# A decoder trunk on one core: the first stage written out as one fixed sequence, and the first gate's products in two halves

## The chip, the core and the metric

The kernel runs on one core of a Trainium2 chip. TensorE (PE) multiplies, VectorE (DVE), ScalarE (ACT) and GpSimd (POOL) work on tiles, SyncE (SP) issues most of the transfers. The metric is the time of one execution on the device in microseconds (us), the median of several runs.

## The reference

Two layers, each with one mixer of three groups of heads side by side; x is 1024 tokens by 1024 channels in f32. What matters here is the beginning of a layer:

```python
mod = c_act @ w_mod + b_mod                      # c_act = SiLU(c), 1024 -> 3 * 1024
shift, scale, gate = jnp.split(mod[:, None, :], 3, axis=-1)
h = rms_norm(x, pre_gain) * (1.0 + scale) + shift
proj = h @ w_in                                  # columns of three groups of heads
...                                              # window attention, retention, gated linear attention
y = jnp.concatenate([a_out, r_out, g_out], axis=-1) @ w_out
return x + gate * rms_norm(y, post_gain)
```

Before any projection of the first layer can be multiplied, shift and scale must be there, and with them h for at least one tile of tokens.

## The kernel before

Tokens are cut into eight tiles of 128 (t), channels into eight of 128 (k). Every f32 operand of a projection is held as a high part and a low part (hi, lo); a product is three passes over the channels, hi by hi, lo by hi and hi by lo, so that a tile with one unit of 256 columns is 24 matmuls. The unit "gg" (the gate of the linear attention) carries 16 more columns, "ga", and has 272; "rg" is the gate of the retention. `project` makes a product, `do_gates` goes through gg and rg for a pair of tiles.

PE issues its instructions in the order in which the program emits them. The other engines' queues are ordered by a scheduler, except where `issue_after` holds an instruction behind another. A planner's clock (`clk`) decides what the program emits next: each matmul adds its cost (columns / 2400, at least 0.107 for 128 stationary columns; 0.109 for an f32 transpose), a generator (`job`) yields a delay and goes on at the first `pump` after it, and `await_flag` moves the clock on where something isn't due yet. The delays stand in the table `L`; `pump` is called every 7 matmuls.

The first stage (`mod_first`, with `between`) works on shift and scale of layer 0 in two halves of 512 channels (hh). For each half ten transfers bring the weights of shift (`wm[0]`) and scale (`wm[1]`), 4 MB for a half. Shift is a row product on PE (line 165 by `mult`, 128x512 operands with one stationary column); scale is summed on VectorE over eight k (L326, L328). `finish` turns both into columns: four matmuls with the summed scale, four with the copied row (L337), each as two instructions, then L309 to L311. Between the two halves stand the loading and splitting of gg (L527 hi on ScalarE, L533 lo on GpSimd, L540 and L541 for ga), and `pre` for tiles 0 and 1 with `early=True`: squares (L651), sum and power for the root (L640, L634, L635 on GpSimd), x times root (L666), eight transposes on PE (L180), modulation (L698 on ScalarE, L700 on VectorE), high part (L704) and low part (L687 or L708). `finish` of the first half is called within the second half's loop, at k = FIN = 1.

After it the jobs for tiles 2 and 3 (with a delay `L["pf1"]` = 6.35 ahead of their transposes) and 4 to 7 (`pre_first`: `L["pf3"] + L["pf2"] * (t - 4)` ahead of their squares, then `pre1` = 7.44 ahead of their transposes) are started, rg is loaded (after x of tiles 2 and 3 in SP's queue; hi on VectorE, lo on VectorE and for the last quarter on GpSimd), and `layer(0)` begins with `do_gates`: gg and rg for tiles 0 and 1, then for 2 and 3, and so on. A tile's product waits for its flag `hT`, which `pre` sets 3.0 after its last step.

Of the kernel before, what the change touches and what calls it, by code (L numbers as in the profile page):

```python
# [10 lines left out]
F32 = mybir.dt.float32  # L11
# [6 lines left out]
P = 128  # L18
# [75 lines left out]
def trunk(ctx: ExitStack, tc: tile.TileContext, ins, cst, out):  # L94
# [200 lines left out]
    def mod_first(rws, between):  # L295
        for j in range(2):
            mod_tile(0, j)
        rc = []
        shift, gain = modc[(0, 0)], modc[(0, 1)]

        def finish(hh, row, acc):
            pc = mm()
            for b in range(4):
                mult(pc[:, 4 + b:5 + b], acc[:, b * P:(b + 1) * P], ones[:, 0:1], True, True)
            for b in range(4):
                mult(pc[:, b:b + 1], row[0:1, b * P:(b + 1) * P], ones[0:1, 0:1], True, True)
            ks = slice(4 * hh, 4 * hh + 4)
            col = small(4)
            V.tensor_tensor(col, pc[:, 4:8], rc[1][:, ks], ALU.add)  # L309
            V.scalar_tensor_tensor(gain[:, ks], col, 1.0, rc[1][:, 8 + 4 * hh:12 + 4 * hh], ALU.add, ALU.mult)  # L310
            V.tensor_tensor(shift[:, ks], pc[:, 0:4], rc[0][:, ks], ALU.add)  # L311
            flag(("modh", 0, hh), 0.0)

        late = None
        for hh in range(2):
            wm = [wp.tile([P, KT, 512], F32, name=nm("wm")) for _ in range(2)]
            acc = t2()
            row = gp.tile([1, 512], F32, tag="acc", name=nm("row"), bufs=1)
            pm = mm()
            for k0, k1 in ((0, 2), (2, 4), (4, 6), (6, 7), (7, 8)):  # L320
                for j in range(2):
                    nc.sync.dma_start(wm[j][:, k0:k1, :], w_mod[0, j, hh, :, k0:k1, :])
            between(hh, -1)
            for k in range(KT):
                if k == 0:
                    V.tensor_scalar(acc, wm[1][:, k], c_act[:, k:k + 1], None, ALU.mult)  # L326
                else:
                    mark[2] = V.scalar_tensor_tensor(acc, wm[1][:, k], c_act[:, k:k + 1], acc, ALU.mult, ALU.add)  # L328
                mult(pm[0:1, :], c_act[:, k:k + 1], wm[0][:, k], k == 0, k == KT - 1)
                if hh == 0 and k == 3:  # L330
                    rc.extend(mod_rows_t(r_) for r_ in rws)
                if late is not None and k == FIN:
                    pump()
                    finish(0, *late)
                    pump()
                between(hh, k)
            A.activation(row, pm[0:1, :], AF.Copy)  # L337
            if hh == 0:
                late = (row, acc)
        finish(1, row, acc)  # L340
        pump()

    def mod_third(l, j):
# [164 lines left out]
    def load(l, name, first=None):  # L508
# [11 lines left out]
        def conv(kc, st):  # L520
            hi, lo = (wt[:, a, 2 * kc:2 * kc + 2, 0:256] for a in range(2))
            if name[0] == "o" and kc == 3:
                A.activation(hi, st, AF.Copy, scale=gnc[:, l:l + 1])
                V.scalar_tensor_tensor(lo, st, gnc[:, l:l + 1], f(hi), ALU.mult, ALU.subtract)
            else:
                if first == 0:
                    A.activation(hi, st, AF.Copy)  # L527
                elif first == 1:
                    V.tensor_copy(hi, st)
                else:  # L530
                    copy(f"whi{kc}", hi, st)
                e = G if first == 0 or name[0] == "o" and kc == 2 else eng(f"wlo{kc}")
                e.tensor_tensor(lo, st, f(hi), ALU.subtract)  # L533
            if kc == 3:
                if name == "gg":
                    gt = wt[:, :, :, 256:272]
                    st = t1()
                    sg = st[:, 0:128].rearrange("p (k n) -> p k n", k=KT)
                    nc.sync.dma_start(sg, w_ga[l])
# [4 lines left out]
        for kc in range(KT // 2):  # L544
            if first is not None:
                conv(kc, *issue(kc))
            else:
                request(l, 1, lambda kc=kc: issue(kc), lambda st, kc=kc: conv(kc, st))
# [83 lines left out]
    def rstd_of(ss, w, scale, eps):  # L632
        r = small(w)
        V.tensor_scalar(r, ss, scale, eps, ALU.mult, ALU.add)  # L634
        G.tensor_tensor(r, r, mhalf[:, :w], ALU.pow)  # L635
# [9 lines left out]
    mark = [None] * 4  # L645
    eb = []
# [7 lines left out]
    def pre(l, t, xt, early=False, soon=False):  # L654
# [12 lines left out]
        yield 0.5 if early else L["pf1"] if soon else lat("pre1", l)  # L667


        at = {}  # L670

        def turn(kt, bank, i):
            at[kt] = bank[:, i * P:(i + 1) * P]
            transp(at[kt], xn[kt // 4][:, kt % 4 * P:(kt % 4 + 1) * P], ident)

        if early:
            if not eb:
                eb.extend((aux(), aux()))
            x = aux()
            for kt in range(KT):  # L680
                turn(kt, x if kt < 4 else eb[kt // 6], kt if kt < 4 else 2 * t + kt % 2)
        late = []
        for j in range(2):
            yield (0.0, ("modh", l, j))
            if late:
                with tc.issue_after(mark[2].ins):
                    V.tensor_tensor(*late.pop(), ALU.subtract)  # L687
            if not early:
# [1033 lines left out]
```

## Time and profile before

| | |
|---|---|
| median of three runs | 998.06 us (997.43 to 999.33) |
| profiled execution | 996.31 us, span 994.6 us |
| granted TensorE clock, mean | 0.991 |
| busy: PE, DVE, ACT, POOL | 965.7, 683.2, 409.3, 246.3 us |
| moved by DMA | 148.77 MB, 150 GB/s over the span |

The span is from the first to the last instruction of the profiled execution; what lies around it is 1.7 us. Rows of the timeline give the start and the length in us, then engine, line, operation, tiles written and read, form, count, and in brackets the idle time of the engine before it and what ended that. Rows of the stretches give the length, then the busy time and the count of PE, PE's weight loads, DVE, ACT and POOL, then the granted clock, the share of the DMA engines and GB/s. Line 165 is the helper for every matmul, line 180 the one for every transpose, so the tiles tell which it is.

### The profile page before, as it was taken

How to read it: one execution, taken by the hardware profiler on the slowest of the kernel's cores; microseconds unless marked ns; L12 is line 12 of the kernel's file. 1: busy time of each engine (PE TensorE's matmuls, PEld its weight loads, DVE VectorE, ACT ScalarE, POOL GpSimd, SP SyncE). 2: the span in 40 equal slices, each digit the busy share in tenths (PEclk: the TensorE clock that was granted, in tenths of full speed). 3: DMA queues.
4: the chain of work that ended last, by engine and by line, in shares of the span. 5: the costliest groups of instructions: out<-in, count | busy, mean ns of one | idle time of the engine just before them, and what ended most of it. 6: DMA issues, size and time to landing. Idle time of an engine off the chain costs nothing.

```text
span 994.6 us, 19641 instructions
## 1 busy us (share of the span) xinstructions
PE 965.7 (97%) x7133; PEld 824.3 (83%) x7133; DVE 683.2 (69%) x1679; ACT 409.3 (41%) x1152; POOL 246.3 (25%) x310
## 2 busy tenths in 40 slices
PE   5899999999999999999999999999999999999996
PEld 1599999888998777778889999988999877777785
DVE  3779857677766777664677286775766577567876
ACT  2477312233332656632555332133333257574222
POOL 2322001233310234420124101113322034545000
PEclk8899999999999999999999999999999999999999
DMA  9843513523135355587555241352122434378883
GB/s 321 290 138 97 159 44 115 177 86 121 61 100 166 91 157 168 170 274 239 189 170 171 69 150 38 118 157 83 53 93 86 127 91 133 112 235 266 267 262 139
DMA packets 112305, 148.77 MB, mean 150 GB/s; under 512 B 12065, under 2 KB 63821, under 8 KB 112209
## 3 DMA queue, kind: packets, MB, share of 16 engines
q1 hardware_dynamic: 106512, 137.96, 44.5%
q10 hardware_dynamic: 5696, 9.56, 2.6%
q8 instruction: 56, 0.92, 0.4%
q14 instruction: 41, 0.33, 0.1%
HBM read 109.20 MB, written 36.18 MB: 146 GB/s over the span
## 4 chain that ended last, share of the span: by engine, by line
PE 80%; DVE 7%; DMA 7%; issue 2%; POOL 1%; ACT 1%; SPq 0%; ACTq 0%; POOLq 0%; DVEq 0%
PE mm L165 61%; PE aux L165 14%; PE aux L180 5%; DMA st<-in_w_in_dram 2%; POOL sm L635 1%; DMA t<-aoS 1%; DMA st<-in_w_last_dram 1%; DMA xk<-in_x_dram 1%; DVE arena L533 1%; DMA a<-mixS 1%; DVE t L1248 0%; DVE t L328 0%; DMA t<-in_x_dram 0%; DMA t<-xs 0%; DMA mixS<-t 0%
## 5 line engine op out<-in xcount | busy, mean ns | idle before, releaser
L165 PE MATMUL mm<-arena 128*128 128x256 f32 (+2 forms) x1824 | 299.9, 318 | 1.8 <-ACT arena L704 1.8
L165 PE MATMUL mm<-arena,arena 128*128 128x256 f32 (+2 forms) x1824 | 298.2, 316 | 0.0
L165 PEld LDWEIGHTS mm<-arena 128*128 128x128 f32 x1824 | 255.5, 191 | 26.0 <-issue 3.3
L165 PEld LDWEIGHTS mm<-arena,arena 128*128 128x128 f32 x1824 | 252.2, 188 | 24.3 <-issue 3.7
L635 POOL TENSOR_TENSOR sm<-sm,mhalf 128x1 f32<-128x1 f32 (+1 forms) x64 | 55.8, 872 | 335.9 <-DVE sm L634 317.8
L165 PE MATMUL mm<-arena,mx 128*128 128x512 f32 (+1 forms) x564 | 130.6, 387 | 0.5 <-ACT kept L1341 0.5
L165 PEld LDWEIGHTS mm<-arena,mx 128*128 128x128 f32 x564 | 101.4, 188 | 24.7 <-issue 1.9
L149 ACT ACTIVATE t<-aux 128x256 f32<-128x256 f32 (+2 forms) x124 | 55.8, 468 | 73.8 <-PE aux L180 62.2
L149 ACT ACTIVATE arena<-st 128x512 fp32r<-128x512 f32 x94 | 56.2, 627 | 53.2 <-DMA st<-in_w_in_dram 19.4
L929 POOL TENSOR_TENSOR smx<-smx,sm 128x512 f32<-128x512 f32 x32 | 36.1, 1129 | 125.7 <-DVE sm L928 118.0
L533 POOL TENSOR_TENSOR arena<-st,arena 128x512 fp32r<-128x512 f32 x31 | 42.7, 1378 | 79.7 <-ACT arena L149 72.9
L533 DVE TENSOR_TENSOR arena<-st,arena 128x512 fp32r<-128x512 f32 x77 | 58.0, 775 | 5.2 <-ACT arena L149 3.3
L925 ACT ACTIVATE smx<-smx,sm 128x129 f32<-128x129 f32 x128 | 49.9, 393 | 25.9 <-DVE sm L922 25.7
L364 DVE SCALAR_TENSOR_TENSOR acc<-st,c_act,acc 128x512 f32<-128x512 f32 x60 | 46.7, 778 | 16.9 <-DMA st<-in_w_mod_dram 16.5
L180 PE MATMUL aux<-c_ident,t 128*128 128x128 f32 (+1 forms) x292 | 48.2, 282 | 5.4 <-DVE t L666 5.0
L180 PEld LDWEIGHTS aux<-c_ident,t 128*128 128x128 f32 (+1 forms) x292 | 35.0, 144 | 12.4 <-DVE t L666 6.9
L698 ACT ACTIVATE t<-aux,mod,mod 128x128 f32<-128x128 f32 x68 | 25.9, 459 | 43.0 <-DVE t L1248 18.1
L165 PEld LDWEIGHTS aux<-t,mx 32*128 32x128 f32 (+1 forms) x896 | 39.5, 187 | 3.9 <-issue 2.1
L973 ACT ACTIVATE t<-aux 128x256 f32<-128x256 f32 x32 | 12.3, 383 | 73.6 <-PE aux L165 65.0
L165 PE MATMUL aux<-t,mx 32*128 32x32 f32 (+1 forms) x896 | 40.7, 272 | 0.0
L920 DVE COPY_PREDICATED smx<-c_curmask,aux 128x256 f32<-128x256 int32 x64 | 25.4, 446 | 19.5 <-ACT smx L149 17.2
L1248 DVE SCALAR_TENSOR_TENSOR t<-t,sm,t 128x512 f32<-128x512 f32 x32 | 24.0, 780 | 18.2 <-DMA t<-in_x_dram 10.8
(224 smaller groups left out, 1387.7 us busy)
## 6 DMA issues: line engine op xcount, KB each, us to landing
st<-in_w_in_dram SPq DMA_DIRECT2D x96, 256.0 KB, 3.8
st<-in_w_mod_dram SPq DMA_DIRECT2D x64, 256.0 KB, 3.1
mx<-mixS SPq DMA_DIRECT2D x20, 512.0 KB, 4.9
mixS<-t SPq DMA_DIRECT2D x72, 128.0 KB, 3.7
st<-in_w_last_dram SPq DMA_DIRECT2D x36, 256.0 KB, 3.8
wm<-in_w_mod_dram SPq DMA_DIRECT2D x12, 512.0 KB, 7.0
t<-in_x_dram SPq DMA_DIRECT2D x24, 256.0 KB, 4.9
t<-tabS SPq DMA_DIRECT2D x16, 256.0 KB, 4.6
```

Of the source, the lines that this page charges most:

```text
L149: A.activation(dst, src, AF.Copy)
L165: T.matmul(dst, lhsT, rhs, start=start, stop=stop)
L180: T.transpose(dst, src, idn)
L364: V.scalar_tensor_tensor(acc, wt, c_act[:, k:k + 1], acc, ALU.mult, ALU.add)
L533: e.tensor_tensor(lo, st, f(hi), ALU.subtract)
L635: G.tensor_tensor(r, r, mhalf[:, :w], ALU.pow)
L698: A.activation(hf[:, ks], at[kt], AF.Identity, scale=gain, bias=shift)
L920: V.copy_predicated(sv, curmask.unsqueeze(1).to_broadcast((P, 2, P)), pv[:, :, n // P - 1, :])
L925: A.activation(sm[:, h, :], sm[:, h, :], AF.Exp, bias=mx[:, h:h + 1], accum_out=sums[:, h:h + 1])
L929: eng("pn").tensor_tensor(sm[:, :, 0:128], sm[:, :, 0:128], rs.unsqueeze(2).to_broadcast((P, 4, P)), ALU.mult)
L973: A.activation(sq, po, AF.Square)
L1248: V.scalar_tensor_tensor(xt[j], yg[j], r, xt[j], ALU.mult, ALU.add)
```

## The change

The first stage becomes a function `first`, and stands in a region in which VectorE, ScalarE, GpSimd and SP, too, issue in the order in which the program emits them (`ORDERED`). Its steps are small functions, called one after the other: loads of half 0, gg, ga, half 1, then rg, then x of tiles 2 and 3 on SP; sums and row products in pairs of k; squares and normalisation of tiles 0 and 1 among them; tile 0's transposes ahead of the row products of k = 6, 7, tile 1's behind the first four column matmuls. The row is copied ahead of three of the four high parts of gg. All low parts of gg, of ga and of rg are GpSimd's; rg's high parts are two on ScalarE and two on VectorE, the latter after the second half's low parts. The low parts of the first half of the channels stand among the sums of the second half.

In `do_gates` the first pair's gg products are made in two halves of the channels: channels 0 to 3 of tile 0 and of tile 1 in two PSUM tiles, then channels 4 to 7 of each. `project` waits for the flag `hT` only where its last channel is among them, as before.

The delays are others: 7.0 and 8.5 for tiles 2 and 3 (`pf2`, `pf3`), 17.3 + 4.16 (t − 4) for the others (`pf4`, `pf5`); the flag `hT` of tiles 0 and 1 is set 2.6 after the last step, rg's flag 3.0 after. Three memsets on GpSimd (those of `acc` and of the two tiles in `gla_tiles`) are held behind the last power of tiles 2 and 3.

```diff
-    def mod_first(rws, between):
...
             if j == 2:
-                G.memset(acc, 0.0)
+                with tc.issue_after(mark[0].ins):
+                    G.memset(acc, 0.0)
...
-        G.tensor_tensor(r, r, mhalf[:, :w], ALU.pow)
+        mark[1] = G.tensor_tensor(r, r, mhalf[:, :w], ALU.pow)
...
-        yield L["pf3"] + L["pf2"] * (t - 4)
+        yield L["pf4"] + L["pf5"] * (t - 4)
         yield from pre(0, t, xt)
...
+    def first(wp):
...
+        def rest(t, j):
+            hi, lo = halves(t, j)
+            V.tensor_tensor(lo, hv[(t, j)], f(hi), ALU.subtract)
...
+        def wlo(n, kc, st):
+            G.tensor_tensor(w[n][:, 1, 2 * kc:2 * kc + 2, 0:256], st, f(w[n][:, 0, 2 * kc:2 * kc + 2, 0:256]),
+                            ALU.subtract)
+
+        mod_load(0)
+        gst = list(issue("gg"))
+        sg = ga_load(0)
+        mod_load(1)
+        sums(0, 0, 1)
+        rowp(0, 0, 1)
+        sums(0, 2, 3)
+        rowp(0, 2, 3)
+        sq(0)
+        rc = [mod_rows_t(r_) for r_ in rws]
+        rowp(0, 4, 5)
+        r0 = rstd2(ss[0])
+        norm(0, r0)
+        sq(1)
+        turn(0)
+        sums(0, 4, 5)
+        r1 = rstd2(ss[1])
+        sums(0, 6)
+        rowp(0, 6, 7)
+        sums(0, 7)
+        norm(1, r1)
+        whi("gg", 0, gst[0], A)
+        wlo("gg", 0, gst[0])
+        row_out(0)
+        pc = cols_a(0)
+        turn(1)
+        for kc in (1, 2, 3):
+            whi("gg", kc, gst[kc], A)
+            wlo("gg", kc, gst[kc])
+        gt = w["gg"][:, :, :, 256:272]
+        A.activation(gt[:, 0], sg, AF.Copy)
+        G.tensor_tensor(gt[:, 1], sg, f(gt[:, 0]), ALU.subtract)
+        cols_r(0, pc)
+        flag(("w", 0, "gg"))
+        modulate(0, 0)
+        modulate(1, 0)
+        rowp(1, 0, 1)
+        sums(1, 0, 1)
+        rest(0, 0)
+        rowp(1, 2, 3)
+        sums(1, 2, 3)
+        rest(1, 0)
+        rgen = issue("rg")
+        rst = [next(rgen) for _ in range(4)]
         for t in (2, 3):
+            load_x(t, xe[t], nc.sync)
+        rowp(1, 4, 5)
+        sums(1, 4, 5)
+        rowp(1, 6, 7)
+        sums(1, 6, 7)
+        row_out(1)
+        pc = cols_a(1)
+        yield
+        w["rg"] = unit(0, "rg")
+        for kc in (0, 1):
+            whi("rg", kc, rst[kc], A)
+            wlo("rg", kc, rst[kc])
+        cols_r(1, pc)
+        for t in range(2):
+            modulate(t, 1)
+        for t in range(2):
+            rest(t, 1)
+            flag(("hT", 0, t), 2.6)
+        for kc in (2, 3):
+            whi("rg", kc, rst[kc], V)
+            wlo("rg", kc, rst[kc])
+        flag(("w", 0, "rg"), 3.0)
+
+    with tc.manual_schedule(engines=ORDERED):
+        with tc.tile_pool(name="first", bufs=1) as wp:
+            steps = first(wp)
+            next(steps)
+        ap = ctx.enter_context(tc.tile_pool(name="big1", bufs=1))
+        arenas.append(ap.tile([P, 4 * SLOT], F32R, name="arena1"))
+        for _ in steps:
+            pass
+        for t in (2, 3):
+            job(pre(0, t, xe[t], f"pf{t}"))
         pump()
...
         def do_gates(name, p):
             w = used(l, name)
+            halved = {}
+            if l == 0 and p == 0 and name == "gg":
+                for t in range(2):
+                    halved[t] = mm()
+                    project(halved[t][:, 0:272], l, t, w, 272, range(KT // 2))
             for t in (2 * p, 2 * p + 1):
-                pg = mm()
+                pg = halved.get(t) or mm()
                 if name == "gg":
-                    project(pg[:, 0:272], l, t, w, 272)
+                    project(pg[:, 0:272], l, t, w, 272, range(KT // 2 if t in halved else 0, KT))
...
-L = {..., "pf3": 13.2, "pf1": 6.35, "pf2": 4.16, ...}
+L = {..., "pf2": 7.0, "pf3": 8.5, "pf4": 17.3, "pf5": 4.16, ...}
+ORDERED = {mybir.EngineType.DVE, mybir.EngineType.Activation, mybir.EngineType.Pool, mybir.EngineType.SP}
-FIN = 1
```

More of the change, by code (lines that the diff above doesn't have):

```diff
@@ L293, in mod_tile @@
         modc[(l, j)] = cp.tile([P, KT], F32, name=nm(f"mod{j}"), tag=f"mod{j}")
-    def mod_first(rws, between):
[L296 to L341, printed above, removed]
     def mod_third(l, j):
@@ L666, in pre @@
                 V.tensor_scalar(xn[j], xt[j], r, None, ALU.mult)
[L667 to L682, printed above, removed]
+        yield L[soon] if soon else lat("pre1", l)
         for j in range(2):
             yield (0.0, ("modh", l, j))
[L685 to L688, printed above, removed]
[L689 to L691 removed]
+            x = aux()
+            for k in range(4):
+                kt = 4 * j + k
+                transp(x[:, k * P:(k + 1) * P], xn[j][:, k * P:(k + 1) * P], ident)
             hf = t2()
```

157 lines of the change are left out of this document (101 added, 56 removed).

## The prediction

> **What bounds the kernel now.** I read the page first, then the chain of work that ended last, the timeline of TensorE, one-microsecond stretches, and single tiles.
>
> ```profile
> span 994.6 us, 19641 instructions
> ...
> PE 965.7 (97%) x7133; PEld 824.3 (83%) x7133; DVE 683.2 (69%) x1679; ACT 409.3 (41%) x1152; POOL 246.3 (25%) x310
> ...
> PE   5899999999999999999999999999999999999996
> ...
> PEclk8899999999999999999999999999999999999999
> ```
>
> TensorE is the bound, with 97% of the span. Only the first two of the forty slices (24.9 us each) have room: there PE is not full and the granted clock is below full speed. What the change can save lies in the first 50 us; after that it can only move PE's instructions, and a wait that it puts in there costs in full. The chain through that stage (start, length, what):
>
> ```profile
> 25.72 0.59 ACT row L337
> ...
> 27.06 1.25 DVE arena L541
> 28.32 1.88 DVE t L326
> ...
> 34.97 0.76 DVE t L328
> ...
> 35.77 2.04 PE mm L165 x16
> ```
>
> VectorE sums the second half of the modulation's weights (L326, then seven L328), but not as they land. It stands behind L541, the low part of the gate's last 16 columns, which waits for ScalarE, which is behind the copy of the row (L337). Then L326 itself takes 1.88 us, while GpSimd is in a memset (start and length in the timeline):
>
> ```profile
> 28.11 1.80 POOL L791 MEMSET mx<- 128x2048 f32 x1
> ```
>
> The last sum ends at 35.73, 16 small products turn sums and row into columns (2.04), and the first gate's products start. TensorE up to there and from there (start, length, line, tiles, count):
>
> ```profile
> 12.75 1.88 PE L165 MATMUL mm<-wm,c_act 128*1 128x512 f32 x4
> ...
> 29.29 5.31 PE L165 MATMUL mm<-wm,c_act 128*1 128x512 f32 x12
> ...
> 37.73 0.77 PE L165 MATMUL mm<-arena 128*128 128x272 f32 x4
> 40.31 6.01 PE L165 MATMUL mm<-arena 128*128 128x272 f32 x27 [1.80 <-ACT arena L704]
> 46.16 1.03 PE L180 MATMUL aux<-c_ident,t 128*128 128x128 f32 x8
> 47.71 1.09 PE L180 MATMUL aux<-c_ident,t 128*128 128x128 f32 x8 [0.52 <-DVE t L666]
> 48.55 2.37 PE L165 MATMUL mm<-arena 128*128 128x272 f32 x17
> 50.76 5.84 PE L165 MATMUL mm<-arena,arena 128*128 128x256 f32 x48
> 56.44 1.93 PE L165 MATMUL mm<-arena 128*128 128x272 f32 x14
> ...
> 58.23 4.54 PE L165 MATMUL mm<-arena 128*128 128x272 f32 x34
> 62.61 0.99 PE L165 MATMUL mm<-arena,arena 128*128 128x256 f32 x7
> 63.44 1.03 PE L180 MATMUL aux<-c_ident,t 128*128 128x128 f32 x8
> 64.31 0.27 PE L180 MATMUL aux<-c_ident,ga 128*48 128x128 f32 x1
> ...
> 68.09 1.04 PE L180 MATMUL aux<-c_ident,t 128*128 128x128 f32 x8
> ```
>
> After the last row product (34.6) and the columns come four products (the channels 0 to 3 of tile 0), then 1.80 of waiting for the second half's first high part; 27 products that take 5.85 from 40.31 to 46.16, 0.217 each, where 34 of them later take 4.38 from 58.23 to 62.61, 0.129 each; and 0.52 before tile 3's transposes. One-microsecond stretches show why the 27 are slow (after POOL's busy time: the granted clock):
>
> ```profile
> 18.00:19.00 1.00, 1.00 (x8) 0.97 (x7) 1.00 (x5) 0.00 (x0) 0.00 (x0) 0.64 1.01 385
> ...
> 38.00:39.00 1.00, 0.50 (x4) 0.28 (x3) 1.00 (x5) 0.76 (x3) 0.45 (x1) 0.88 0.89 291
> 39.00:40.00 1.00, 0.00 (x0) 0.00 (x0) 1.00 (x4) 1.00 (x4) 0.00 (x0) 0.50 0.78 248
> ...
> 44.00:45.00 1.00, 1.00 (x6) 1.00 (x5) 0.97 (x4) 0.00 (x0) 0.00 (x0) 0.50 0.18 68
> 45.00:46.00 1.00, 1.00 (x7) 1.00 (x7) 0.71 (x3) 0.00 (x0) 0.48 (x1) 0.71 0.00 0
> ```
>
> The clock fell to half at about 38.8 and rose inside 45 to 46. From 34.6 on PE had done only the 16 one-column products and four real ones. It had fallen once before, at about 18.3, and there the last row product had ended at 14.63: 3.7 us without one.
>
> **The change, part by part.** I count at one milestone: the moment at which PE has done the first two tiles' products for both gates (96) and the transposes of tiles 2 and 3 (16). Before it is 56.44, 18.71 after the start at 37.73. At full clock that work takes 48 by 0.129 plus 48 by 0.118 (50.76 to 56.44) plus 2 by 0.87 (63.44 to 64.31 for 8 transposes), 13.6. So 5.1 are lost: idle 1.80 and 0.52, half clock 27 by 0.088, 2.4, and 0.4 of small joints.
>
> Start of the products. L541 moves to GpSimd, the copy of the row moves ahead of three high parts, the memset goes behind a mark, and the sums are queued as the weights land. What is left is the landing. The loads of this tile (count, duration of the issue, first and last start; then issue to landing):
>
> ```profile
> L322 SPq DMA_DIRECT2D wm<-in_w_mod_dram x20: 327/328/666, 1.3 to 25.0; - x20
> ...
> DMA to landing us min/median/max: 6.6/6.8/7.0
> ```
>
> The last piece lands at 25.0 + 7.0 = 32.0. It cannot go sooner: its place in SP's queue is the same, and ahead of it stand the same bytes. Earliest start: 32.0 + one sum 0.76 + 2.04 = 34.8; latest 37.73, if the two low parts of the first half that now stand between the sums hold the sums up. I take 35.9: after the same landing PE still has the row's last product and ScalarE its copy (0.59), which before were ready in time and now are not, and each hand-over takes some 0.1. That is 1.8 sooner. On SP the four loads of the second weight now go ahead of x of tiles 2 and 3, which are thus four 256 KB loads later; their squares ran only from 40.7 on, so this hides.
>
> Halves. PE's order becomes 24 products over channels 0 to 3 of both tiles, then 24 over channels 4 to 7. They add no matmul: 48 either way, in two PSUM tiles instead of one. The first 24 take 24 by 0.129, 3.1, to 39.0; the second half's first high part comes, as before, some 2.6 after the columns (37.73 to 40.31), at 38.5. So the 1.80 of idling goes, covered with 0.5 to spare. If the low parts of the first half were late, the cover would be gone and up to 1.8 come back.
>
> The 0.52 before tile 3. Its normalised x must be there when PE arrives, after 48 products, 21 of the second gate and 8 transposes: 35.9 + 6.2 + 2.5 + 0.9 = 45.5. In the fixed order the power on GpSimd now stands behind four low parts of the second weight:
>
> ```profile
> L533 POOL TENSOR_TENSOR arena<-st,arena 128x512 fp32r<-128x512 f32 x4 | 5.0, 1264 | 1.3 <-ACT arena L527 1.3
> 44.03 0.88 DVE L666 TENSOR_SCALAR t<-mx,sm 128x512 f32<-128x512 f32 x2 [0.44 <-POOL sm L635]
> 45.52 0.60 POOL L635 TENSOR_TENSOR sm<-sm,mhalf 128x1 f32<-128x1 f32 x1 [1.53 <-DVE sm L634]
> ```
>
> Two of the four need casts that come on VectorE after tile 1's last low part, at about 40.2; 2 by 1.26 gives 42.8, tile 2's power 43.4, its x 44.3, tile 3's power 45.2, its x 46.1. So 0.5 remain: no gain here.
>
> Clock. The last row product will end at 32.0 + 5.31/6 = 32.9 or later, so PE's pause in real products shrinks to 3.0 (32.9 to 35.9), and no second one follows. The two falls came after 3.7 and more. Between no loss and the 2.4 of before I take 1.2. Milestone: 35.9 + 13.6 + 0.5 + 1.2 = 51.2, with nothing for joints, against 56.44. That is 5.2; **I count 5.2 gained in the first stage**, at most 6.9 (35.9 + 13.6), at least 1.8 (the 1.80 alone, with start and clock as before).
>
> Now what is put in. The planner's clock decides where tile 4's transposes stand in PE's order. By its costs (0.113 and 0.107 for a product, 0.109 for a transpose) two tiles of both gates are 48 by 0.113 plus 48 by 0.107, 10.6. Before, tile 4 comes at 13.2 + 7.44 = 20.6 after the stage, of which 3.0 were jumped over in waiting for tile 0: after 17.6 of work, and the row at 63.44 stands there, 7 products into the second gate of tile 2. After the change the clock does not jump (24 products are 2.7, over the 2.6 of the new flag), and tile 4 comes at 17.3 + 7.44 = 24.7. But tiles 0 to 3 are through both gates at 2 by 10.6 + 1.7 for 16 transposes + 0.2 = 23.1. So tile 4's transposes stand directly ahead of its own products, with nothing between. PE must wait there for ScalarE and VectorE. What that wait is, by tiles 4, 5 and 6 before, from their transposes on PE (63.44, 68.09, and here 72.89) to their high and low parts:
>
> ```profile
> 65.32 1.50 ACT L698 ACTIVATE t<-aux,mod,mod 128x128 f32<-128x128 f32 x4
> 67.30 1.18 ACT L704 ACTIVATE arena<-t 128x512 fp32r<-128x512 f32 x2
> 67.98 1.29 DVE L708 TENSOR_TENSOR arena<-t,arena 128x512 fp32r<-128x512 f32 x2 [1.01 <-ACT arena L704]
> 72.89 1.03 PE L180 MATMUL aux<-c_ident,t 128*128 128x128 f32 x8
> 74.09 0.68 DVE L708 TENSOR_TENSOR arena<-t,arena 128x512 fp32r<-128x512 f32 x1
> 75.57 0.66 ACT L704 ACTIVATE arena<-t 128x512 fp32r<-128x512 f32 x1
> ```
>
> First high part of tile 6: 72.89 to 76.23, 3.3; of tile 4: 63.44 to about 67.9, 4.5; last low part of tile 4: 69.27, 5.8. Less the transposes' own time, 1.0, PE stands for 2.3 at best and 4.8 at worst. I take 2.8, near the short row, since ScalarE has fewer conversions queued here than tile 4 found. Tile 5 comes at 4.16 after tile 4, 7 products into tile 4's; 17 products, 2.2, lie between it and its own: 3.3 less 1.0 less 2.2, nothing by the short row; by its own long row (68.09 to 74.77, 6.7) it is 3.5. I take nothing. Tiles 6 and 7 have a whole pair's second gate ahead of their use.
>
> **Sum.** 5.2 less 2.8 is 2.4 gained. The profiled execution took 996.31 with a span of 994.6 and would take 993.9. It is 1.75 below the median of the runs shown, 998.06, and below all three. From the median: 998.06 − 2.4 = **995.7**.
>
> **Rivals.** *The tile-4 wait costs nothing*, because high parts come while PE still works: for it, ScalarE and VectorE are ahead by then; against it, PE runs in order and those transposes come last. Then all 5.2 stay, 992.9, or 6.9, 991.2, when the first stage loses nothing to the clock or to tile 3.
>
> *The wait at tile 4 lets the clock fall once more.* The transposes, 1.0, and a wait of 3.5 (tile 4's row) make 4.5 without a product; the fall at 18.3 came after 3.7. It would cost another 2.4, by the 27 products above: 5.2 − 3.5 − 2.4 = −0.7 gained, 998.8. Even the short row's 3.3 is near. [...]
>
> *Slower: the gates wait for the whole chain of tiles 4 and 5.* PE now comes earlier than ScalarE and VectorE are ready for it, and the long rows hold: 4.8 for tile 4 and 3.5 for tile 5, and the clock falls in it, 2.4. Together 10.7 less 5.2 is 5.5 lost, 1003.6. It decides as soon as the waits and the clock pass 7.2. For it: the low parts come last in tile 5's row; against it: only 16 of 24 products of a tile need low parts or the upper channels, so the first 8 lie beside that wait.
>
> *The halves do nothing*, since tile 0's second half is ready as PE gets there: then 1.8 comes back, 997.5, inside the range.
>
> **How the numbers follow.** What a measurement here can tell from no change is about 0.2%, 2 us. Forecast with its own range of 994.0 to 997.5: 0.41, of which 0.31 is faster than 996.1. No wait at tile 4: 0.18, faster. Clock falls again: 0.21, the same. Whole chains: 0.20, slower. That makes faster 0.49, same 0.31, slower 0.20. The range runs from 991.2 (first stage at its best and no wait) to 1001.0, which leaves out the upper half of the slow case.
>
> **What would show it.** Right: the first 272-column product at 35 to 36.5 with 24 in a row; the milestone at 50 to 52.5; an idle PE of 2 to 4 us at about 62 to 66 whose releaser is ScalarE's L698 line or its high part, directly behind 8 transposes. Wrong in the first stage: VectorE's last sum still ends after 35, or the clock is 0.50 for 7 us after 36. Wrong in the second: tile 4's products follow its transposes at once, or PE waits twice, at tiles 4 and 5, for low parts.

## The result, and the profile after

The changed kernel takes **1012.16 us** (median of four runs, 1010.98 to 1013.83) against 998.33 beside it: a ratio of 1.014 [1.0121, 1.0158]. It is 14 us slower; the prediction was 995.7, with a range that ended at 1001.0. The profiled execution took 1010.98.

The page of the changed kernel (busy times; the forty slices, now 25.2 us each):

```profile
span 1009.3 us, 19637 instructions
...
PE 971.7 (96%) x7133; PEld 828.2 (82%) x7133; DVE 687.8 (68%) x1673; ACT 410.9 (41%) x1154; POOL 249.0 (25%) x314
...
PE   6879899999999999999999999999999999999996
...
PEclk9888999999999999999999999999999999999999
```

TensorE has the same 7133 matmuls. Its third and its fifth slice are no longer full: most of the loss lies between 50 and 126 us, behind the stage that was rewritten. Its timeline there (start, length, line, tiles, count, idle time before and what ended it):

```profile
35.04 7.74 PE L165 MATMUL mm<-arena 128*128 128x272 f32 x48
42.62 2.65 PE L165 MATMUL mm<-arena,arena 128*128 128x256 f32 x21
45.10 1.05 PE L180 MATMUL aux<-c_ident,t 128*128 128x128 f32 x8
47.98 1.11 PE L180 MATMUL aux<-c_ident,t 128*128 128x128 f32 x8 [1.83 <-DVE t L613]
48.85 0.60 PE L165 MATMUL mm<-arena,arena 128*128 128x256 f32 x3
53.42 4.61 PE L165 MATMUL mm<-arena,arena 128*128 128x256 f32 x24 [3.97 <-DVE t L1078]
57.87 4.07 PE L165 MATMUL mm<-arena 128*128 128x272 f32 x31
...
69.83 1.05 PE L180 MATMUL aux<-c_ident,t 128*128 128x128 f32 x8
...
73.20 0.76 PE L165 MATMUL mm<-arena,arena 128*128 128x272 f32 x4 [2.21 <-ACT arena L633]
74.93 1.05 PE L165 MATMUL mm<-arena,arena 128*128 128x272 f32 x3 [0.97 <-ACT arena L633]
...
99.72 3.13 PE L165 MATMUL mm<-arena 128*128 128x256 f32 x24 [1.32 <-DVE t L1078]
...
117.57 0.66 PE L180 MATMUL aux<-c_ident,t 128*128 128x128 f32 x4 [2.69 <-DVE t L402]
```

The products begin at 35.04, near the earliest start of the forecast (34.8), and 48 run in one row without the 1.80 of idling. Then come six waits; before had one of 0.52 in the same work. The other engines at the first two of them, and at the one of tile 4 (their timelines; the last line is the kernel before):

```profile
43.59 0.88 DVE L613 TENSOR_SCALAR t<-mx,sm 128x512 f32<-128x512 f32 x2 [1.58 <-POOL sm L583]
...
44.88 0.56 POOL L583 TENSOR_TENSOR sm<-sm,mhalf 128x1 f32<-128x1 f32 x1 [1.32 <-DVE sm L582]
45.84 1.80 POOL L877 MEMSET mx<- 128x2048 f32 x1
...
45.47 2.85 DVE L613 TENSOR_SCALAR t<-mx,sm 128x512 f32<-128x512 f32 x2 [0.74 <-POOL sm L583]
...
48.69 1.50 ACT L627 ACTIVATE t<-aux,mod,mod 128x128 f32<-128x128 f32 x4 [6.98 <-PE aux L180]
...
52.37 0.39 ACT L1076 ACTIVATE t<-mm 128x256 f32<-128x256 f32 x1
...
52.86 0.41 DVE L1078 SCALAR_TENSOR_TENSOR t<-t,mm 128x256 f32<-128x256 f32 x1
...
71.85 0.75 DVE L317 SCALAR_TENSOR_TENSOR acc<-st,c_act,acc 128x512 f32<-128x512 f32 x1 [2.43 <-DMA st<-in_w_mod_dram]
```

```profile
48.40 1.50 ACT L698 ACTIVATE t<-aux,mod,mod 128x128 f32<-128x128 f32 x4 [5.14 <-PE aux L180]
```

- **Tile 3.** The memset of mx, held behind tile 3's power, starts in the middle of tile 3's normalisation (L613): 2.85 for the pair, where tile 2's took 0.88. The transposes wait 1.83.
- **The third PSUM tile.** Products share three PSUM tiles. The second rg product needs the one of tile 0's gg, which the tanh (L1076) and L1078 read out. Both stand behind tile 2's modulation (L627), for which ScalarE had waited 6.98; that modulation starts at 48.69, where it started at 48.40 before. PE stands for 3.97, and the clock is half from 50.0 to 56.9. What ended the 6.98 was not tile 2's own transposes (done at 46.15) but the first four of tile 3 (done at 48.65). In the program as built the modulation writes the buffer from which these read: `t2` has ten buffers, x of tiles 4 to 7 fills eight of them, and tiles 2 and 3 share the other two. It is so in the kernel before as well.
- **Tile 4.** VectorE waits 2.43 for a load of a later job (L317, the sum of the gate's modulation) just before it must modulate tile 4.

I follow the rest by one measure: the start of matmul n less its start in the kernel before, in us. n counts all 7133 from the start of the program, transposes too; n = 83 is the first product of a gate. It was read for every experiment (they are told below; no run has the number E4 or E8).

| kernel | n = 83 | 140 | 180 | 300 | 340 | 560 | 700 | end |
|---|---|---|---|---|---|---|---|---|
| after | −2.7 | −6.2 | 0.8 | 1.5 | 7.9 | 9.3 | 13.7 | 14.6 |
| E1 | −1.7 | −5.2 | 1.8 | 3.4 | 8.3 | 8.0 | 15.2 | 17.1 |
| E2 | −1.3 | −4.8 | 0.2 | 1.6 | 4.1 | 9.5 | 10.1 | 10.5 |
| E3 | −3.2 | −6.7 | −4.9 | 4.9 | 7.4 | 10.7 | 13.7 | 12.7 |
| E5 (before, delay alone) | 0.5 | 0.5 | 0.5 | 0.5 | 8.3 | 8.6 | 13.1 | 12.2 |
| E6 | −0.2 | −5.1 | 3.8 | 4.4 | 5.3 | 5.2 | 14.2 | 15.0 |
| E7 | −1.8 | −6.6 | −0.2 | 0.2 | 1.1 | 4.3 | 13.4 | 15.6 |
| E9 | −1.6 | −1.5 | 2.6 | 3.3 | 4.9 | 15.4 | 17.0 | 18.7 |
| E10 | −0.7 | −4.2 | 0.9 | 2.3 | 3.2 | 6.4 | 14.1 | 16.1 |
| E11 | −0.7 | −4.1 | 0.8 | 2.2 | 2.4 | 3.3 | 3.3 | 3.9 |
| E12 | −2.2 | −7.1 | −2.2 | −0.8 | 0.6 | 1.5 | 1.5 | 4.2 |
| E13 | −0.8 | −4.3 | −4.4 | 6.3 | 7.4 | 8.3 | 8.3 | 7.2 |
| E14 | −1.4 | −6.4 | −6.5 | −6.5 | −1.0 | 0.0 | 0.0 | 0.2 |
| E15 (before, tables alone) | 0.6 | 0.6 | 0.6 | 0.6 | 0.6 | 1.3 | 10.9 | 13.5 |
| E16 | −1.6 | −5.2 | −5.4 | −5.4 | −3.0 | −0.9 | −0.9 | −0.9 |

So the changed kernel is 6.2 ahead after 140 matmuls. It loses 7.0 by n = 180 (tile 3 and the PSUM tile), 0.7 from there to 300, 6.4 at tile 4 (300 to 340), and 5.8 from there to 700, of which 4.4 lie behind 560, where the tables' transposes stand. The 880 us behind that add 0.9.

Each row is one profiled execution. E1, E2, E3, E6, E7 and E9 have the same first stage as after, and their first product starts between 34.51 and 37.48; so leads of single rows that differ by 1 or 2 tell little, and losses between two columns tell more. Most of these executions lie within 2 of their kernel's median, but E3's is 4.3 and E14's 3.3 below it, and E15's 4.9 above.

### The profile page after: what moved, and what is told of

Read it like the earlier page. It is cut to its first block, busy times and chain, and to the rows that moved or that the text cites. A ratio compares the mean times of both kernels' runs of the same rounds, so it can differ in the third digit from the quotient of the medians.

```text
span 1009.3 us, 19637 instructions
## 1 busy us (share of the span) xinstructions
PE 971.7 (96%) x7133; PEld 828.2 (82%) x7133; DVE 687.8 (68%) x1673; ACT 410.9 (41%) x1154; POOL 249.0 (25%) x314
## 4 chain that ended last, share of the span: by engine, by line
PE 75%; DVE 8%; DMA 8%; issue 2%; ACT 2%; POOL 2%; SPq 0%; ACTq 0%; POOLq 0%; DVEq 0%
PE mm L165 57%; PE aux L165 14%; PE aux L180 4%; DMA st<-in_w_in_dram 3%; DVE arena L486 1%; DMA xk<-in_x_dram 1%; POOL sm L583 1%; DMA st<-in_w_last_dram 1%; DMA wm<-in_w_mod_dram 1%; DMA a<-mixS 1%; DVE t L613 0%; DVE st L547 0%; DVE t L1334 0%; DMA st<-in_w_mod_dram 0%; DVE t L1065 0%
## 5 line engine op out<-in xcount | busy, mean ns | idle before, releaser
L165 PE MATMUL mm<-arena,arena 128*128 128x256 f32 (+2 forms) x1824 | 301.6, 319 | 7.1 <-DVE t L1078 4.0
L165 PEld LDWEIGHTS mm<-arena,arena 128*128 128x128 f32 x1824 | 255.5, 191 | 32.1 <-issue 7.8
L583 POOL TENSOR_TENSOR sm<-sm,mhalf 128x1 f32<-128x1 f32 (+1 forms) x64 | 55.4, 866 | 334.6 <-DVE sm L582 312.1
L165 PEld LDWEIGHTS mm<-arena,mx 128*128 128x128 f32 x564 | 101.5, 188 | 25.2 <-ACT kept L1427 1.7
L317 DVE SCALAR_TENSOR_TENSOR acc<-st,c_act,acc 128x512 f32<-128x512 f32 x60 | 47.5, 791 | 18.5 <-DMA st<-in_w_mod_dram 17.9
L486 POOL TENSOR_TENSOR arena<-st,arena 128x512 fp32r<-128x512 f32 x26 | 36.5, 1406 | 80.4 <-ACT arena L149 73.3
L1006 DVE COPY_PREDICATED smx<-c_curmask,aux 128x256 f32<-128x256 int32 x64 | 25.4, 446 | 18.7 <-ACT smx L149 15.2
L627 ACT ACTIVATE t<-aux,mod,mod 128x128 f32<-128x128 f32 x56 | 21.5, 460 | 39.8 <-DVE t L1334 18.9
L1334 DVE SCALAR_TENSOR_TENSOR t<-t,sm,t 128x512 f32<-128x512 f32 x32 | 24.0, 780 | 18.7 <-DMA t<-in_x_dram 11.9
```

The lines of the kernel that those rows point to most:

```text
L165: T.matmul(dst, lhsT, rhs, start=start, stop=stop)
L317: V.scalar_tensor_tensor(acc, wt, c_act[:, k:k + 1], acc, ALU.mult, ALU.add)
L583: mark[1] = G.tensor_tensor(r, r, mhalf[:, :w], ALU.pow)
L627: A.activation(hf[:, ks], x[:, ks], AF.Identity, scale=gain, bias=shift)
L1006: V.copy_predicated(sv, curmask.unsqueeze(1).to_broadcast((P, 2, P)), pv[:, :, n // P - 1, :])
L1334: V.scalar_tensor_tensor(xt[j], yg[j], r, xt[j], ALU.mult, ALU.add)
```

## The experiments

My theory after the result was the place: the new delays put tile 4 and the tables badly against PE's work. The rival was supply: ScalarE and VectorE are late wherever PE asks. The texts on record call them Theory 1 and Theory 2 and say what each would make of the run. Each ratio is to runs of the kernel before on the same chip.

**E1, E2, E3, E5: one part undone, or done alone.**

```diff
E1, on after:  -"pf4": 17.3   +"pf4": 13.2
E2, on after:  +        if l == 0:
               +            mark[0] = mark[1]      # the three memsets behind tile 7's power
                        job(mod_all(l, (2,)))
E3, on after:  first pair's gates inside tc.manual_schedule(engines={ACT, DVE})
E5, on before: -"pf3": 13.2   +"pf3": 17.3
```

> The changed kernel with one number altered: tiles 4 to 7 start 13.2 instead of 17.3 after the first stage, as before. Theory 1 (separate local waits): tile 4's transposes again stand some rg products ahead of tile 4's own gg products, the waits of 2.2 and 1.0 us for its high parts and the half-clock stretch from 73.9 to 80.8 go, and with them the 6.4 us by which the changed kernel falls back there (1.5 behind at product 300, 7.9 behind at product 340): about 1006, at 1005 to 1007. Theory 2 (ScalarE and VectorE cannot deliver sooner, wherever PE asks): the wait turns up one or two tiles later, 1010 to 1013.

1013.47, ratio 1.0164 [1.0141, 1.0186]. The delay alone does not cure it. At n = 340 E1 is where after is, and the tables' transposes wait longer than there (timeline of E1):

```profile
114.73 1.12 PE L180 MATMUL aux<-c_ident,t 128*128 128x128 f32 x4 [5.74 <-DVE t L402]
```

> The changed kernel with the three memsets held behind a later power on GpSimd (the last one of the gates instead of tile 3's). Theory 1: VectorE's normalisation of tile 3 is not stopped by the 1.80 us memset that now starts at 45.84; PE's 1.83 us of waiting at 47.98 goes, all that hangs on tile 3 comes 1.8 sooner, PE's next wait (3.97 at 53.42, for a PSUM tile) ends 1.8 sooner too: about 1010, at 1009 to 1011. Theory 2: the 3.97 grows by what the 1.83 shrinks, 1012 plus or minus 1.

1006.96, 1.01 [1.0083, 1.0118]: about 4 better by the ratios, twice what I expected. Counted from the first product (which starts 1.4 later here than in after), 2.0 of it come by n = 180: PE no longer waits for tile 3's x, though still 4.0 for the PSUM tile. The rest goes through VectorE's queue: the memset of acc, held longer, moves the first L317 from the 93rd to the 145th of VectorE's instructions (before it is the 151st). Its wait of 2.43 ahead of tile 4 is gone, and E2 loses 2.5 from 300 to 340 where after loses 6.4. That gain is lost again by 560 (5.3 against 1.4, behind waits of 1.61 and 1.95), and what stays comes at the tables, where the wait falls from 2.7 to 0.5.

> The changed kernel with ScalarE and VectorE kept in the order of emission through the first pair's gates, so that the tanh and the product that free tile 0's PSUM tile go ahead of tile 2's modulation. Theory 1: PE's 3.97 us of waiting at 53.42 shrinks to under 1 us, and the half clock after it with it: 1007 to 1009. Theory 2: the modulations of tiles 2 and 3 are now the late ones, PE waits as long for their high parts, 1011 to 1013.

1013.52, 1.016 [1.0127, 1.0192]. The wait for the PSUM tile at 53 goes (−4.9 at 180), and comes back as 2.70 for a high part of tile 2 (L633, at 54.92) and 3.66 for a PSUM tile (at 62.83): tanh first is of no use as long as tiles 2 and 3 come no sooner.

> The kernel before with one number altered: tiles 4 to 7 start 17.3 instead of 13.2 after the first stage. By the planner's clock tile 4's transposes then come within the last rg products of tile 3, some 10 products ahead of its own. Theory 1: PE waits there for tile 4's high parts, 1 to 2.5 us, with or without 2.4 us for the clock: 1000 to 1003. Theory 2 (the delays are indifferent, and what costs is the first stage): 998 plus or minus 1.

1009.76, 1.0129 [1.0108, 1.015]: 12 to 13 us by one delay, with the whole old first stage, far above both theories' ranges. From n = 300 on E5 loses as after does. Tile 4's place is thus a cause by itself, enough for 8 at tile 4 and 4.5 at the tables.

**E6, E7, E9, E10: the place put back.** I had the planner's clock jump 3.0 again ahead of the first products:

```diff
E6:  +                clk[0] += 3.0
     +                pump()
     -"pf2": 7.0, "pf3": 8.5, "pf4": 17.3   +"pf2": 10.0, "pf3": 11.5, "pf4": 13.2
E7:  E6 and the edit of E2
E9:  E7, and "for t in range(2)" of the halves becomes "for t in ()"
E10: E7, with x of tiles 2 and 3 ahead of rg on SP, their squares behind the row's copy,
     their powers ahead of rg's low parts, "pf2": 8.6, "pf3": 9.4
```

> The changed kernel with the place of everything behind the first stage put back where it stood against PE's work before: the planner's clock jumps 3.0 ahead of the first products, as it did in waiting for tile 0, and tiles 4 to 7 have 13.2 again, so that tile 4's transposes come after 17.6 of work and the tables' job, too, stands where it stood; tiles 2 and 3 keep their places (10.0 and 11.5 less the jump). Theory 1 (place): of the 14.6 that the changed kernel is behind at the end, 13 come after the 300th matmul and from the places alone; they go, no wait at tile 4 (68 to 75) and none at the tables' transposes (111 to 118), and it ends 1 to 2 behind before: 998 to 1001. Theory 2 (supply): ScalarE and VectorE are late wherever PE asks; the waits turn up at another place, some 6 to 10 behind: 1004 to 1009.

> The kernel with the places put back, and besides the three memsets held until the last power of tile 7, so that none runs beside tile 3's normalisation. Theory 1: the 1.8 before tile 3's transposes goes, but the wait for a PSUM tile at about 53 stays (4.0), and the end is 0.5 to 1.5 better than with the places alone, level with before: 997 to 1000. Theory 2: as without the place, about 1005 to 1007, since the memsets were worth 5 there.

> The kernel with the places put back and the memsets held, but the first pair's gg products made whole, tile 0's 24 and then tile 1's 24, in place of the two halves. Theory 1: PE waits about 1.8 for the second half's high part after 4 products, as before, but tile 0's PSUM tile is complete 12 products sooner; both end at the same wait for tiles 2 and 3, whose x sets that time, so the end moves by less than 0.7. Theory 2: the halves are worth their 1.8: 1.5 to 2.5 slower than with them.

> The kernel with the places put back and the memsets held, and tiles 2 and 3 prepared inside the fixed sequence: x of tiles 2 and 3 ahead of rg on SP, their squares on ScalarE behind the copy of the row, where it is idle (33 to 36.4), their powers on GpSimd ahead of rg's four low parts, and their transposes after 48 and 55 products in place of 62 and 75. Theory 1: the changed kernel lost its lead of 6 because ScalarE began tile 2's modulation no sooner than before (48.7 against 48.4); here it begins at 43 to 45, so 3 to 5 of the lead reach the 180th matmul, and if nothing later takes it, the end is 2 to 5 ahead of before: 993.5 to 996.5. Theory 2: ScalarE and VectorE have that much to do from 43 to 75 that the lead is gone by tile 4: 998 or more.

E6 1011.65, 1.0149 [1.0123, 1.0175]; E7 1012.76, 1.0155 [1.0124, 1.0186]; E9 1015.12, 1.0188 [1.0166, 1.021]; E10 1013.64, 1.0174 [1.0144, 1.0204]. Every forecast by Theory 1 fell, and E6 and E7 lie above the ranges of Theory 2 too. Yet the first half of Theory 1 held: little is lost at tile 4 (E6, E7 and E10 0.9 from 300 to 340). The great loss comes at the tables: 8 to 9 at once in E6, E7 and E10, by waits of 6.8, 7.0 and 6.3 with half clock behind them: seven products took 1.70 (E6, at 116.01) and 1.64 (E7, at 115.42) where they took 0.99 at 95, and ten took 2.46 (E10, at 114.47). Holding the memsets longer gained nothing in E7: there they run beside the normalisation of a later tile (its rows stand in the last section), and PE waits 1.57 for that.

E9 tells what the halves are worth: without them PE waits after four products, and E9 is 3.0 behind E7 at n = 300, as its Theory 2 said (a lower clock, 0.982 over its span and 0.987 over E7's, is part of it: the 44 products behind the wait took 8.42, 0.19 each, where 0.13 is full speed).

```profile
39.03 8.42 PE L165 MATMUL mm<-arena 128*128 128x272 f32 x44 [2.14 <-ACT arena L747]
```

E10 shows a second price of GpSimd's low parts (VectorE's and GpSimd's timelines of E10, then of E12, where the low parts are on VectorE):

```profile
41.08 2.95 DVE L728 TENSOR_SCALAR t<-mx,sm 128x512 f32<-128x512 f32 x2
...
41.03 2.71 POOL L768 TENSOR_TENSOR arena<-st,arena 128x512 fp32r<-128x512 f32 x2 [0.53 <-ACT arena L765]
```

```profile
39.98 1.67 DVE L728 TENSOR_SCALAR t<-mx,sm 128x512 f32<-128x512 f32 x4
```

Two normalisations take 2.95 beside GpSimd's subtraction, four take 1.67 without it.

**E15: the tables alone.** Why the tables? In E1, E6, E7 and E10 the copy that feeds the tables' first transposes stands 25 to 27 places behind the tables' last step (L395) in VectorE's queue; before it stands 2 places behind that step (L442 there). My jump was lost on that job: its delay (tb1) was now counted from behind the jump, so that the copy was emitted 50.7 of work after the first product (in E1, which has no jump, 50.7 too) in place of 47.3, just late enough for the scheduler to put other work ahead. E15 is the kernel before with this alone:

```diff
-"tb1": 24.5   +"tb1": 28.0
```

> The kernel before, with one number changed: the tables' job starts at 28.0 in place of 24.5, so that the first copy for the tables' transposes is emitted 50.7 of work after the first product, as in the changed kernel with pf4 13.2; VectorE's queue then has it 24 instructions behind the tables' last step in place of 2. First stage, tiles 2 to 7 are as before. Theory 1 (queue): the same wait as there, 5.5 to 7 at the tables' transposes at about 105 and half clock behind it: 7 to 9 slower, 1003.5 to 1006. Theory 2 (supply): VectorE has the same work at the same time as before, the transposes are asked for 3.3 later too, and nothing or up to 1 is lost: 996 to 998.

1004.81, 1.0089 [1.0058, 1.012]. VectorE's timeline of the kernel before, then VectorE's and PE's of E15:

```profile
92.27 0.43 DVE L442 TENSOR_SCALAR sincos<-sincos 128x512 f32<-128x512 f32 x1
93.16 0.42 DVE L449 COPY t<-sincos 128x512 f32<-128x512 f32 x1
```

```profile
96.39 0.42 DVE L442 TENSOR_SCALAR sincos<-sincos 128x512 f32<-128x512 f32 x1
...
108.71 0.41 DVE L449 COPY t<-sincos 128x512 f32<-128x512 f32 x1
...
109.18 1.12 PE L180 MATMUL aux<-c_ident,t 128*128 128x128 f32 x4 [6.88 <-DVE t L449]
```

The table is ready at 96.8 and copied at 108.7. The wait and the fall of the clock behind it (seven products took 1.70 at 112.22, 0.99 at 91.69) cost about 9, by queue order alone; supply, the rival, is refuted for this part of E1, E6, E7 and E10. The changed kernel itself has its first copy 2 places behind the last step; its loss at the tables is told in the next section. (The profiled execution was the longest of E15, and loses 2.6 more late in the program, where nothing was changed.)

**E11, E12, E13: tables' place and memsets mended.**

```diff
E11: E6 with pump() ahead of the jump, "tb1": 23.0; memsets of mx behind a small GpSimd copy that
     reads tile 3's normalised x, memset of acc behind tile 7's power
E12: E10 likewise; rg's four low parts on VectorE, behind the normalisations of tiles 2 and 3
E13: E12 and the order of E3
```

> The changed kernel with every place behind the first stage put back: the clock jumps 3.0 ahead of the first products, tiles 4 to 7 have 13.2, and the tables' job has 23.0 in place of 24.5, so that the first copy for the tables' transposes is emitted 47.3 of work after the first product, as before; in the two kernels with places put back so far it was emitted 50.7 after it, and VectorE's queue then had it 24 instructions behind the tables' last step instead of 2. The memsets of mx stand on GpSimd behind tile 3's normalisation, that of acc behind tile 7's power. Theory 1 (queue): the 6.8 to 7.0 of waiting at the tables' transposes (104 to 111, with 1.9 of half clock) were that queue order; they go, and the 0.2 behind at the 300th matmul is what is left, with up to 2 of smaller waits: 996.5 to 1000. Theory 2 (supply): VectorE gets there as late, since it has 4 more to do or to wait for from 56 to 92; 3 to 7 stay at the tables: 1001 to 1006.

> The same places, and tiles 2 and 3 prepared inside the fixed sequence (x ahead of rg on SP, squares on ScalarE behind the row's copy, powers ahead of everything else on GpSimd, transposes after 48 and 55 products); rg's four low parts are on VectorE behind both normalisations, not on GpSimd, where two of them made a pair of normalisations take 2.9 in place of 0.9. Theory 1: normalisations by 43, tile 2's modulation at 44 to 45 in place of 48.7; the lead at the 180th matmul is 2 to 4, less what the wait for a PSUM tile takes (up to 4, if ScalarE still puts both tiles' modulation ahead of the first tanh), and nothing is lost at the tables: 993 to 998. Theory 2: 998 to 1003, the lead is gone by tile 4.

> The same kernel, with ScalarE and VectorE kept in the order of emission through the first pair's gates, so that the tanh of the first products stand ahead of the modulation of tiles 2 and 3 and the third PSUM tile comes free. Theory 1: no wait at 50 to 54 for a PSUM tile, and tiles 2 and 3 are in time, as they are prepared 4 sooner: 2 to 5 ahead at the 180th matmul and at the end: 992 to 996. Theory 2: as in the first kernel with this order, the wait moves to the first product of tile 2 (3 to 5) and the end is no better than 998.

E11 1001.21, 1.0037 [1.0014, 1.006]; E12 1000.41, 1.0041 [1.0022, 1.0061]; E13 1004.87, 1.0079 [1.0062, 1.0097]. In E11 the copy follows the table at once, and the wait is gone:

```profile
93.11 0.42 DVE L395 TENSOR_SCALAR sincos<-sincos 128x512 f32<-128x512 f32 x1
93.63 0.43 DVE L402 COPY t<-sincos 128x512 f32<-128x512 f32 x1
...
100.40 0.60 PE L180 MATMUL aux<-c_ident,t 128*128 128x128 f32 x4
```

By the ratios that is 10 of the 14 us, with the new first stage as it is. E11 differs from E7 in three things (tb1, the two places of memsets), and I did not separate them; by the table of lags, 9 came at the tables and 2.3 from 340 to 560. E11 ended 1.2 above Theory 1's range and in Theory 2's, though the wait that Theory 2 kept is gone; E12 ended in Theory 2's, and E13 far from Theory 1's, as Theory 2 said. E12 prepares tiles 2 and 3 four us sooner, yet waits 3.9 for the PSUM tile. In E13 emission order makes VectorE wait for a small load that SP issues behind x of tiles 4 to 7, and tile 2's low part and the second half of its modulation with it:

```profile
52.96 0.17 DVE L872 TENSOR_SCALAR gnc<-gnc 128x2 f32<-128x2 f32 x1 [6.57 <-DMA gnc<-in_gla_norm_gain_dram]
```

**E14, E16: the PSUM tile freed in time.**

```diff
E14, on E12: tile 2's modulation on ScalarE under tc.issue_after(last tanh);
             the loads of gnc and of the sinks ahead of x of tiles 4 to 7
E16, on E14: rq's high parts on ScalarE under tc.issue_after(last tanh)
```

> The kernel with every place put back and tiles 2 and 3 prepared in the fixed sequence, and besides ScalarE's modulation of tile 2 held behind the tanh of the first two products, so that the PSUM tile of tile 0 comes free before rg of tile 1 asks for it; the small loads of the norm gain and the sinks stand ahead of x of tiles 4 to 7 on SP, since VectorE's steps on them now come earlier. That kernel without it waited 3.9 for the PSUM tile and had half clock from 48.9 to 55.7. Theory 1: both go, the lead of 7 at the 160th matmul stays past the 180th (4 to 7), and, since VectorE's and ScalarE's work for tiles 4 to 7 and the tables does not move up by as much, 1 to 4 of it are left at the end: 993 to 997. Theory 2 (supply): the lead is lost again by the 340th, and the end is where that kernel's was, 999 to 1001.

999.84, 1.0029 [1.0009, 1.0049]; Theory 2's number. But the lead of 6.5 now lasts to n = 300, and most of it goes in one wait (timelines of PE, then of ScalarE, then of VectorE):

```profile
44.92 5.21 PE L165 MATMUL mm<-arena,arena 128*128 128x256 f32 x41
...
67.52 2.33 PE L165 MATMUL mm<-arena,arena 128*128 128x272 f32 x14 [3.67 <-DVE t L1093]
```

```profile
63.65 0.63 ACT L149 ACTIVATE arena<-st 128x512 fp32r<-128x512 f32 x1 [0.99 <-DMA st<-in_w_in_dram]
...
64.25 0.92 ACT L1091 ACTIVATE t<-mm 128x256 f32<-128x256 f32 x3
```

```profile
66.16 0.88 DVE L619 TENSOR_SCALAR t<-t,sm 128x512 f32<-128x512 f32 x2 [2.08 <-POOL sm L583]
66.96 0.41 DVE L1093 SCALAR_TENSOR_TENSOR t<-t,mm 128x256 f32<-128x256 f32 x1
```

The 41 products of rg run on without a gap. At 64 three tanh come at once: they had stood behind rq's high parts, one of which waited for its load. The tanh are done at 65.17; the last 1.8 before L1093 are VectorE's, which had a normalisation ahead of it and waited 2.08 for GpSimd's power (L583).

> The kernel with tile 2's modulation behind the tanh, which kept its lead of 6.5 up to the 300th matmul and then waited 3.7 (63.9 to 67.5) for a PSUM tile, with half clock from 69.0 to 72.4; ScalarE had three high parts of rq's weight, one of them waiting for its load, ahead of the tanh of tile 3. Here each of these high parts is held behind the tanh that is emitted before it. Theory 1 (order of ScalarE's queue): that wait and the half clock behind it go, and 3 to 6 of the lead are left at the end: 990.5 to 994. Theory 2 (supply): the lead is lost at the next tile or at the tables, since the tables' copies on VectorE do not come sooner: 995 to 998.

995.9, 0.9987 [0.9975, 0.9999] (12 runs, 17 of before): the only version that is ahead of both kernels, 15 ahead of after by the ratios and 1.3 ahead of before, less than the 2 that the prediction held to be tellable. The same wait is 2.15 now and the clock stays full behind it (eight transposes took 1.03 at 68.90, in E14 1.91 at 69.65); the lead shrinks from 5.4 to 0.9 in that and smaller waits up to 92. That is again Theory 2's number: what is left of the lead is lost to a late ScalarE and VectorE, tile by tile.

## Why the prediction was wrong

- **Start of the products**: 35.9 forecast, 35.04 measured. Right: the seven profiles with this first stage start at 34.51 to 37.48, 35.9 in the mean, so the 0.9 by which this one was sooner is scatter.
- **Halves**: right. No idling, 48 in one row; E9 prices them at 3.0 rather than 1.8, clock included.
- **The 0.52 before tile 3**: 1.83. The chain of powers was right (the last one ended at 45.44, forecast 45.2); the step that failed took 0.88 for each pair of normalisations. Behind it stood the memset that the change itself had moved there, and which I had counted only as gone from the sums.
- **Clock**: 1.2 forecast. The 48 products at 7.74, with half clock from 36.4 to 39.8, are 1.5 over full speed, near the forecast; the second fall, at 50.0 in the wait that ended at 53.42, was not in it.
- **The milestone**, 51.2 forecast, 57.87 measured, 1.4 behind before: here the sum failed. 35.9 + 13.6 + 0.5 + 1.2 is PE's own work and the waits that the trace of before showed. I asked what would be late next only for tile 3's x, not for the PSUM tile (3.97), which before came free while PE still had products. ScalarE's modulation of tile 2 did not start sooner, 48.69 against 48.40, because it hangs on tile 3's transposes, and so on the memset, too (in E2 it starts 2.0 sooner, counted from the first product). Neither half of the cure was enough alone: E12 starts it at 44.11 and PE still waits 3.89, E3 puts the tanh ahead and PE waits elsewhere; with both (E13 and E14) the wait is gone. More buffers of `t2`, which would part the two tiles, were not tried.
- **Tile 4**: 2.8 forecast; 2.21 and 0.97 measured, but 6.4 lost, with half clock from 73.9 to 80.8. The wait was right, the clock behind it left out of the sum, and the rival "lets the clock fall once more" was the true case here (3.5 + 2.4 against 6.4); part of the 6.4 may be VectorE's wait of 2.43 for a load, which no term had.
- **Nothing behind tile 7** was in the forecast; 5.8 were lost there. All later work hangs on the same clock. In after that clock jumps 5.6 in waiting for the flags of tiles 4 and 5, as it expects PE to stand there, and the tables' first copy is emitted 44.0 of work after the first product in place of 47.3; VectorE reaches it 7 later than before all the same. PE does not yet wait for that one. It waits 2.69 for the second copy, which starts 12 later than before and stands 41 places behind the tables' last step in place of 32 (VectorE's timelines of after, then of before):

```profile
100.24 0.42 DVE L402 COPY t<-sincos 128x512 f32<-128x512 f32 x1
...
117.10 0.41 DVE L402 COPY t<-sincos 128x512 f32<-128x512 f32 x1
```

```profile
105.11 0.41 DVE L449 COPY t<-sincos 128x512 f32<-128x512 f32 x1
```

E5 shows the loss at tile 4 and this one, with the same 41 places, without any new first stage; E15 shows that queue order at the tables can cost still more. The slower rival of the prediction had the right sign, but neither the size (10.7 at tiles 4 and 5, where 6.4 were lost, with no wait of 3.5 at tile 5) nor the cause.

In short: the sum counted the waits that the old trace showed and put at nothing those that a sooner PE would run into, for the PSUM tile (3.97 and a fall of the clock), and everything behind tile 7 (5.8).

Open: how the loss at tile 4 in after divides between the delay and the load that L317 waits for (E2 points to some 3.9 of 6.4 for the latter, but loses it again by 560). E12's last 2.4 are lost at one place, a wait of 2.25 for ScalarE's `kept` at 935.3 (0.54 before); E11 and E15 lose 1.4 and 2.8 there. Nothing was changed there, and why the wait differs stays open.

## What to carry to other kernels

A lead on the bounding engine is worth only what the engines that feed it can follow: look for the instruction on each of them that does not start sooner, for what it waits (here a buffer that another tile still held), and for the PSUM tiles that stand behind it. A delay in a planner is measured against its clock; when a change takes a jump out of that clock, everything placed by it moves, jobs far behind the edit too. And where a scheduler orders the queues, a place that moves by 3 of 1000 us can put a copy behind 24 instructions, so the queue's order around each hand-over is to be read, not only the busy shares.

## What the hardware showed

VectorE's tensor_scalar on SBUF took longer beside a long GpSimd instruction: 0.88 for a pair alone, 2.85 beside a memset of 1.80 (after), 2.95 beside a subtraction of 2.71 (E10), and in E7 4.60 beside two memsets:

```profile
75.46 4.60 DVE L613 TENSOR_SCALAR t<-t,sm 128x512 f32<-128x512 f32 x2 [0.34 <-POOL sm L583]
...
75.84 3.56 POOL L877 MEMSET mx<- 128x2048 f32 x2
```

The excess is 2.0, 2.1 and 3.7, against 1.8, 2.7 and 3.6 of GpSimd's instructions. What holds VectorE up there was not shown. Four modulations from PSUM took 1.37 (L629, from 49.14) beside a memset that ran from 48.43 to 50.24, and 1.36 (L745, from 36.44) without one.

In the kernel before the clock was at half from 18.3 to 25.1, from 38.8 to 45.6 and from 991.1 on; in after from 22.7 to 26.1, 36.4 to 39.8, 50.0 to 56.9, 73.9 to 80.8, 118.3 to 121.7 and from 1005.8 on. In after it fell within PE's wait of 3.97 (before 53.42) and behind waits of 2.21 (before 73.20) and 2.69 (before 117.57), and stayed full behind one of 1.32 (before 99.72). E16's 2.15 left it full, and in E14 it fell at 69.0, 1.5 after the products had resumed from a wait of 3.67.
